# Causal mask of layer A's attention: added by VectorE in PSUM in place of TensorE, with the second sum of each step issued behind the next step's mask

## The chip, the cores and the metric

The kernel runs on one core of a Trainium2 chip. The metric is the device time of one execution in microseconds (us); the time shown is the median of several runs. The engines have short names in the profile: PE is TensorE's matmul, PEld its weight load, DVE is VectorE, ACT is ScalarE, POOL is GpSimd and SP is SyncE, whose queue issues the DMAs here.

## The reference

A two-layer decoder trunk over 2048 tokens of width 1024 in float32. Layer A is forgetting attention: 16 heads of 64, causal softmax with a cumulative log forget gate as bias. Then come one shared K/V projection and layer B, a sliding-window attention with sinks. Only layer A's attention is touched by the change; cut to what matters:

```python
def fox_attention(q, k, v, log_f):
    c = jnp.cumsum(log_f, axis=1)
    ...
    def block(args):                      # 128 queries at a time
        idx, qi, ci = args
        logits = einsum('bqhd,bkhd->bhqk', qi, k) * HEAD_DIM ** -0.5
        logits = logits + ci[..., :, None] - c_k[..., None, :]
        causal = k_pos[None, :] <= q_pos[:, None]
        logits = jnp.where(causal, logits, -jnp.inf)
        p = jax.nn.softmax(logits, axis=-1)
        return einsum('bhqk,bkhd->bqhd', p, v)
# layer A: h = h + (o * silu(gate)) @ w_out_a
```

## The kernel before

Every float32 product is made of high and low parts: a value is split into a rounded part and the rest, and a product is the sum of two or three matmuls. So PE has several matmuls of 512 columns for each tile of each projection, and the other engines make the splits.

Layer A's attention is the function `attention_a`. Work is cut into 64 units, one for each head and each chunk `ch` of 512 queries (4 chunks). Scores are held transposed, with 128 keys on the partitions and up to 512 queries along the columns. A unit of chunk `ch` has 2*ch + 2 steps, and each step `p` treats two blocks of 128 keys; a head has 20 steps and all heads 320. In most steps both blocks are seen by all 512 queries. The last two steps of a unit hold the diagonal: step 2*ch has blocks of 512 and 384 columns, each with a triangle of 128 columns to be masked, and the last step has 256 and 128 columns in one PSUM tile, with two triangles masked together.

A step runs like this. `scores` issues two matmuls for each block into PSUM tiles `sc` (L995 and L996; three banks). In the two diagonal steps a further matmul adds the mask: the identity in bf16, `identb`, times the triangle `mask_s`, which holds -1e30 above the diagonal (L1005 twice in step 2*ch, L1001 once, 256 columns wide, in the last step). ACT takes the exponentials into `pf` (L1011, L1002; tag `st`, four slots), casts them to the high part (L1014), and POOL subtracts that for the low part (L1015). For the softmax's denominator the exponentials are summed over the keys on DVE: a PSUM bank `ac` (one slot) starts as a copy of the unit's first block (L1018, ACT), and each further block is added to it by DVE (L1024), the two blocks of a step one after the other. Behind the last step of a unit `sums` reduces `ac` (L912, DVE), and five steps later `recips` (L921 to L928) forms reciprocals.

Around this other work is threaded. `values` (L1039, PE) runs three steps behind the scores, in one PSUM bank `pa`, with the high and the low part. `max_pieces` computes the running row maxima of the following head: PE writes a piece into one of two PSUM banks `mx` (L950), and DVE reduces it (L963) or, on the diagonal, adds a bf16 mask in place and reduces (L958). There are 40 pieces a head, two in each step, one before the scores and one behind them. `gate` is a filler: it feeds the matmuls of the gate projection (L1081, bank `pb`) whose weights come by DMA through SP into `wr`, and whose products are finished on DVE and ACT (L1092 to L1094).

The order in the text is the program's order. The framework plans each engine's queue: an instruction that its cost model takes as ready may go ahead of one that is listed earlier and is not ready; among ready ones the earlier listed goes first. `keep_in_program_order` pins an instruction behind all listed before it on its engine. Each engine runs its queue in order.

Of the kernel before, what the change touches and what calls it, by code (L numbers as in the profile page):

```python
# [14 lines left out]
BF16 = mybir.dt.bfloat16  # L15
# [3 lines left out]
ALU = mybir.AluOpType  # L19
# [4 lines left out]
P = 128  # L24
# [76 lines left out]
def f_(ap):  # L101
    return ap.bitcast(F32)
# [51 lines left out]
class Trunk:  # L154
# [56 lines left out]
    def constants(self):  # L211
        nc, cp, a = self.nc, self.const, self.a

        def select(view, src, pattern, base, cm, fill):
            nc.gpsimd.affine_select(
                out=view, in_=src, pattern=pattern, compare_op=ALU.is_ge,
                fill=fill, base=base, channel_multiplier=cm,
            )

        def tile_(name, shape, dt=F32):  # L220
            return cp.tile(shape, dt, name=name, tag=name)

        idle = self.sb("sq", [P, CH], F32R)
        nc.vector.memset(f_(idle), 0.0)
        ps = self.ps("pb", [P, CH])
        for i in range(IDLE):
            self.tc.keep_in_program_order(
                nc.tensor.matmul(ps, idle[:, :P], idle, start=i == 0, stop=i == IDLE - 1)
            )

        self.ones = tile_("ones", [P, P])
        nc.gpsimd.memset(self.ones, 1.0)
        self.tri = tile_("tri", [P, P])
        select(self.tri, self.ones, [[1, P]], 0, -1, 0.0)
        self.ident = tile_("ident", [P, P])
        select(self.ident, self.tri, [[-1, P]], 0, 1, 0.0)

        self.fold = tile_("fold", [P, 32])
        nc.vector.tensor_tensor(self.fold, self.ident[:, :32], self.ident[:, 32:64], ALU.add)
        for c in (64, 96):  # L240
            nc.vector.tensor_tensor(self.fold, self.fold, self.ident[:, c : c + 32], ALU.add)
        nc.vector.tensor_single_scalar(self.fold, self.fold, 2.0, ALU.mult)
        self.identb = tile_("identb", [P, P], BF16)
        nc.vector.tensor_copy(self.identb, self.ident)

        self.mask_s = tile_("mask_s", [P, P], BF16)
        nc.gpsimd.memset(self.mask_s, 0.0)
        select(self.mask_s, self.mask_s, [[1, P]], 0, -1, NEG)

        self.band = tile_("band", [P, 2, P], BF16)  # L250
        nc.gpsimd.memset(self.band[:, 0], 0.0)
        select(self.band[:, 0, :], self.band[:, 0, :], [[-1, P]], 0, 1, NEG)
        nc.vector.tensor_tensor(self.band[:, 1], self.tri, self.ident, ALU.subtract)

        self.loads = []
        warm = tile_("warm", [P, 1])
        nc.scalar.activation(warm, self.ones[:, :1], AF.Sqrt)

        def vector(name, n, views):
            t = tile_(name, [P, n])  # L260
            for rows, src in views:
                self.loads.append((t[rows], src))
            return t

        def column(name, src, n):
            return vector(name, n, [(slice(0, P), src.rearrange("(t p) -> p t", p=P))])

        def pair_column(name, src):
            col = src.rearrange("(p o) -> p o", o=1)
            return vector(name, 1, [(slice(0, HD), col), (slice(HD, P), col)])  # L270

        def row(name, src, n):
            return vector(name, n, [(slice(0, P), src.to_broadcast([P, n]))])

        self.g_a = column("g_a", a["norm_a_g"][0], NDT)
        self.bf = row("bf", a["b_forget"], H)
        self.g_qa = pair_column("g_qa", a["qnorm_a_g"][0])
        self.g_ka = pair_column("g_ka", a["knorm_a_g"][0])
        self.g_b = column("g_b", a["norm_b_g"][0], NDT)
        self.g_kv = column("g_kv", a["kv_norm_g"], NDT)  # L280
        self.g_qb = pair_column("g_qb", a["qnorm_b_g"][0])
        self.g_kb = pair_column("g_kb", a["knorm_b_g"])
        self.sink = row("sink", a["sinks"], H)
        self.gq16 = row("gq16", a["qnorm_b_g"][:, :ROT], ROT)
# [579 lines left out]
    def attention_a(self, op):  # L864


        nc, tc, d = self.nc, self.tc, self.d
# [15 lines left out]
        heads, state = {}, {}  # L883
        units = [(h, ch) for h in range(H) for ch in range(NCH)]
# [24 lines left out]
        def sums(u):  # L909

            h, ch = units[u]
            nc.vector.tensor_reduce(  # L912
                part[h // 2 % 2][:, h % 2, ch, :], state[u][0].rearrange("p (b i) -> p b i", i=32),
                AX.X, ALU.add, apply_transpose=True,
            )
# [55 lines left out]
        def blocks(ch, p):  # L971

            if p < 2 * ch:
                return [(2 * p, 0, 512, 0), (2 * p + 1, 0, 512, 512)]
            if p == 2 * ch:
                return [(2 * p, 0, 512, 0), (2 * p + 1, 128, 384, 512)]
            return [(2 * p, 256, 256, 0), (2 * p + 1, 384, 128, 256)]

        def scores(n, u, p):
            h, ch = units[u]  # L980
            ka, kb, qa, qb, v, _ = heads[h]
            bl = blocks(ch, p)
            diag, last = p >= 2 * ch, p > 2 * ch

            tiles = [self.ps("sc", [P, CH]) for _ in range(1 if last else 2)]
            tw = bl[1][3] + bl[1][2]
            pf = self.sb("st", [P, 1024])
            ph, pl = pht[:, n % 4, :], plt[:, n % 4, :]
            for n_, (k, q0, w, off) in enumerate(bl):
                qs = slice(ch * CH + q0, ch * CH + q0 + w)  # L990
                ks = slice(k * P, (k + 1) * P)
                ps = tiles[0 if last else n_]
                o0 = off if last else 0
                o = ps[:, o0 : o0 + w]
                nc.tensor.matmul(o, ka[:, ks], qa[:, qs], start=not (last and n_), stop=False)  # L995
                nc.tensor.matmul(o, kb[:, ks], qb[:, qs], start=False, stop=not diag)  # L996

            if last:
                o = tiles[0].rearrange("p (b q) -> p b q", b=2)[:, :, :P]
                m = self.mask_s.unsqueeze(1).to_broadcast([P, 2, P])  # L1000
                nc.tensor.matmul(o, self.identb, m, start=False, stop=True)  # L1001
                nc.scalar.activation(pf[:, :tw], tiles[0][:, :tw], AF.Exp, scale=HD**-0.5)  # L1002
            else:
                for n_, ps in enumerate(tiles if diag else ()):
                    mm = nc.tensor.matmul(  # L1005
                        ps[:, :P], self.identb, self.mask_s, start=False, stop=True
                    )
                    if n_:
                        tc.keep_in_program_order(mm)
                for ps, (k, q0, w, off) in zip(tiles, bl):  # L1010
                    nc.scalar.activation(  # L1011
                        pf[:, off : off + w], ps[:, :w], AF.Exp, scale=HD**-0.5
                    )
            nc.scalar.copy(ph[:, :tw], pf[:, :tw])  # L1014
            nc.gpsimd.tensor_tensor(pl[:, :tw], pf[:, :tw], f_(ph[:, :tw]), ALU.subtract)  # L1015
            if p == 0:
                state[u] = [self.ps("ac", [P, CH]), None]
                nc.scalar.copy(state[u][0], pf[:, :CH])  # L1018
            acc = state[u][0]
            for n_, (k, q0, w, off) in enumerate(bl):  # L1020
                if p == 0 and n_ == 0:
                    continue
                a_ = acc[:, q0 : q0 + w]
                nc.vector.tensor_tensor(a_, a_, pf[:, off : off + w], ALU.add)  # L1024
            if last:
                sums(u)
            return (u, p, ph, pl)

        def values(item):
# [123 lines left out]
        for n, (u, p) in enumerate(steps):  # L1153
# [26 lines left out]
            if n in PREP_AT:  # L1180
                op.load(PREP_AT.index(n), ("qn", "wh", "qn", "wl"))
                op.prepare(PREP_AT.index(n), nc.gpsimd)
        op.load(2, ("qn", "wh", "qn", "wl"))
        gate_bank, weight_slots = "mx", cycle(["st", "wr"])
        for item in pending:
# [463 lines left out]
```

## Time and profile before

| | us |
|---|---|
| median of 3 runs (2434.35 to 2436.96) | 2435.06 |
| the profiled execution | 2432.95 |
| its span, first to last instruction | 2431.0 |
| PE busy, of the span | 2406.9 |
| DVE busy | 1730.6 |
| ACT busy | 1260.0 |
| POOL busy | 997.5 |

The granted TensorE clock was 1.00. Busy time of an engine is the time in which at least one of its instructions has its span open; matmuls overlap, so PE's busy time is no measure of how near it is to its peak, and the distance between the starts of two neighbours says what the first takes of the engine. A row of a timeline gives start, length, engine, line, operation and tiles, with a count where neighbours were merged, and in brackets the idle time ahead of it. A row of the chain or of the waits names a line of the kernel as printed above. A row of windows gives the stretch, its length, the busy time of PE, PEld, DVE, ACT and POOL with the number of instructions in brackets, the clock and the DMA's share and rate.

### The profile page before, as it was taken

The numbers are of one execution on the slowest core, as the hardware profiler recorded it, in microseconds if no ns is written. First come the engines' busy times: TensorE is split into PE (matmuls) and PEld (weight loads), VectorE is DVE, ScalarE is ACT, GpSimd is POOL, SyncE is SP. The second block draws the span as 40 slices with busy tenths as digits, with TensorE's granted clock in tenths as the row PEclk, the third lists the DMA queues.
The fourth block names the chain that finished last, engine by engine and source line by source line (L and its number), as shares of the span: only waits on it lengthen the run. The fifth ranks groups of instructions, "written<-read, shape, count | busy, mean of one in ns | idle before, by whom it ended". The sixth has DMA issues, their size and how long they took to land.

```text
span 2431.0 us, 36257 instructions
## 1 busy us (share of the span) xinstructions
PE 2406.9 (99%) x11960; PEld 2027.7 (83%) x11960; DVE 1730.6 (71%) x4086; ACT 1260.0 (52%) x2504; POOL 997.5 (41%) x642
## 2 busy tenths in 40 slices
PE   9999999999999999999999999999999999999999
PEld 7888899987888788888888878888888888788887
DVE  7756657735999888899988865556666523777775
ACT  5433324323878778777878761135332312555554
POOL 0000000011878777777878852200011000477775
PEclk9999999999999999999999999999999999999999
DMA  6656555677654755575466559965433425655552
GB/s 185 208 168 190 154 155 166 197 235 232 179 165 127 211 155 147 150 219 167 127 196 178 166 153 312 299 225 162 120 107 105 139 72 157 179 178 180 180 180 74
DMA packets 351484, 419.25 MB, mean 172 GB/s; under 512 B 64896, under 2 KB 248224, under 8 KB 345120
## 3 DMA queue, kind: packets, MB, share of 16 engines
q1 hardware_dynamic: 351296, 416.93, 57.5%
q8 instruction: 95, 1.56, 0.3%
q14 instruction: 93, 0.76, 0.1%
HBM read 265.30 MB, written 151.40 MB: 171 GB/s over the span
## 4 chain that ended last, share of the span: by engine, by line
PE 90%; DVE 4%; DMA 3%; ACT 2%; issue 1%; POOL 1%; SPq 0%; ACTq 0%; DVEq 0%; POOLq 0%
PE b L774 30%; PE pa L1039 10%; PE pb L1081 7%; PE b L1266 5%; PE pb L1479 5%; PE sc L995 5%; PE sc L996 5%; PE mx L950 5%; PE pb L737 3%; PE b L737 3%; PE pa L1409 2%; PE b L1330 2%; PE pb L358 1%; DVE wl L502 1%; PE pa L358 1%
## 5 line engine op out<-in xcount | busy, mean ns | idle before, releaser
L774 PE MATMUL b<-wh,big 128*128 128x512 f32 (+3 forms) x2560 | 772.0, 375 | 0.7 <-ACT wh L501 0.7
L1015 POOL TENSOR_TENSOR big<-st,big 128x1024 fp32r<-128x1024 f32 (+1 forms) x320 | 655.5, 2068 | 238.7 <-ACT big L1014 157.2
L774 PEld LDWEIGHTS b<-wh,big 128*128 128x128 f32 x2560 | 470.9, 188 | 72.0 <-ACT wh L501 2.5
L774 PE MATMUL b<-wl,big 128*128 128x512 f32 (+3 forms) x1280 | 474.4, 371 | 0.8 <-DVE wl L502 0.8
L1024 DVE TENSOR_TENSOR ac<-ac,st 128x512 f32<-128x512 f32 (+3 forms) x576 | 353.1, 613 | 51.0 <-ACT st L1011 25.5
L1011 ACT ACTIVATE st<-sc 128x512 f32<-128x512 f32 (+1 forms) x512 | 273.4, 582 | 117.7 <-PE sc L996 50.1
L1039 PE MATMUL pa<-big 128*128 128x512 f32 (+3 forms) x1280 | 319.2, 366 | 0.6 <-POOL big L1015 0.6
L1014 ACT CAST big<-st 128x1024 fp32r<-128x1024 f32 (+1 forms) x320 | 295.2, 923 | 8.5
L774 PEld LDWEIGHTS b<-wl,big 128*128 128x128 f32 x1280 | 241.5, 189 | 37.4 <-DVE wl L502 5.2
L1039 PEld LDWEIGHTS pa<-big 128*128 128x128 f32 x1280 | 229.4, 190 | 38.4 <-POOL big L1015 1.9
L963 DVE TENSOR_REDUCE mt<-mx 128x1 f32<-128x384 f32 (+1 forms) x360 | 214.7, 599 | 30.5 <-PE mx L950 28.1
L510 ACT ACTIVATE sq<-b,r 128x512 f32<-128x512 f32 (+2 forms) x128 | 77.7, 607 | 304.2 <-PE b L774 304.2
L995 PE MATMUL sc<-big 128*128 128x512 f32 (+3 forms) x640 | 233.1, 368 | 1.1 <-DVE st L557 1.1
L996 PE MATMUL sc<-big 67*128 67x512 f32 (+3 forms) x640 | 229.8, 367 | 0.0
L950 PE MATMUL mx<-big 66*128 66x512 f32 (+2 forms) x600 | 225.3, 380 | 0.2
L1081 PE MATMUL pb<-wh,wr 128*128 128x512 f32 x488 | 177.6, 396 | 3.4 <-DMA wr<-wg 3.3
L512 DVE TENSOR_REDUCE sm<-sq 128x8 f32<-128x512 f32 (+2 forms) x128 | 74.9, 585 | 141.3 <-ACT sq L510 141.1
L874 POOL MEMSET rot<- 128x512 bf16 x1 | 0.5, 524 | 419.8 <-PE pb L358 419.8
L1378 POOL TENSOR_TENSOR big<-big,tri 128x1024 fp32r<-128x1024 f32 x60 | 143.8, 2397 | 69.2 <-DVE big L1375 64.3
L958 DVE CUSTOM_DVE_ANT_0 mx<-mx,rot 128x384 f32<-128x384 f32 (+2 forms) x240 | 147.1, 618 | 17.5 <-PE mx L950 16.2
L995 PEld LDWEIGHTS sc<-big 128*128 128x128 f32 x640 | 121.9, 190 | 22.7 <-DVE st L557 1.5
L996 PEld LDWEIGHTS sc<-big 67*128 67x128 f32 x640 | 122.1, 191 | 19.2
(285 smaller groups left out, 4131.3 us busy)
## 6 DMA issues: line engine op xcount, KB each, us to landing
wr<-wg SPq DMA_DIRECT2D x62, 512.0 KB, 4.5
va<-st SPq DMA_DIRECT2D x32, 512.0 KB, 4.7
ka<-st SPq DMA_DIRECT2D x64, 256.0 KB, 3.8
ut<-big SPq DMA_DIRECT2D x16, 1024.0 KB, 7.0
big<-ka SPq DMA_DIRECT2D x16, 1024.0 KB
big<-qa SPq DMA_DIRECT2D x16, 1024.0 KB, 8.2
qb<-st SPq DMA_DIRECT2D x64, 256.0 KB, 3.8
big<-qb SPq DMA_DIRECT2D x16, 1024.0 KB, 6.3
```

What stands on the lines that cost most here:

```text
L774: nc.tensor.matmul(ps[:, :n], u[tb // 4][:, dt, us], W[k][dt], start=(dt == 0 and i == 0), stop=(dt == NDT - 1 and i == 2),)
L950: mm = nc.tensor.matmul(ps, qb[:66, i * P : (i + 1) * P], kb[:66, k0:k1], start=True, stop=True,)
L958: nc.vector.tensor_tensor_reduce(out=ps, in0=ps, in1=mask_m[:, 512 - w :], scale=1.0, scalar=NEG, op0=ALU.add, op1=ALU.max, accum_out=f_(o),)
L963: nc.vector.reduce_max(o, ps, axis=AX.X)
L995: nc.tensor.matmul(o, ka[:, ks], qa[:, qs], start=not (last and n_), stop=False)
L996: nc.tensor.matmul(o, kb[:, ks], qb[:, qs], start=False, stop=not diag)
L1011: nc.scalar.activation(pf[:, off : off + w], ps[:, :w], AF.Exp, scale=HD**-0.5)
L1014: nc.scalar.copy(ph[:, :tw], pf[:, :tw])
L1015: nc.gpsimd.tensor_tensor(pl[:, :tw], pf[:, :tw], f_(ph[:, :tw]), ALU.subtract)
L1024: nc.vector.tensor_tensor(a_, a_, pf[:, off : off + w], ALU.add)
L1039: nc.tensor.matmul(pv[:, q0 : q0 + w], v[:, k, :], src[:, off : off + w], start=(p == 0 and n_ == 0 and i == 0), stop=(last and n_ == 1 an ...
L1081: nc.tensor.matmul(ps, w[:, dt // 2 % 2, wk, dt % 2, :], us[dt][uk], start=(dt == 0 and i == 0), stop=(dt == NDT - 1 and i == 2),)
```

## The change

The two mask matmuls of step 2*ch and the one of the last step go, and with them `identb` and the copy that made it. In their place DVE adds `mask_s` to the score tiles in PSUM, in place, ahead of the exponentials: two additions of 128 columns, and one over both triangles (256 columns). The second block's sum of a step, and the unit's reduction `sums`, are no longer issued in the step itself but put on a list, `to_add`, which `add_up` empties in the next step behind its masks and ahead of its exponentials; what is left after the last step is added after the loop. The first block's sum stays in its own step. The step's second score matmul now ends its accumulation where the mask did.

```diff
-        self.identb = tile_("identb", [P, P], BF16)
-        nc.vector.tensor_copy(self.identb, self.ident)
...
+        to_add = []
+
+        def add_up():
+
+            for u, p, bl, pf in to_add:
+                k, q0, w, off = bl[1]
+                a_ = state[u][0][:, q0 : q0 + w]
+                nc.vector.tensor_tensor(a_, a_, pf[:, off : off + w], ALU.add)
+                if p > 2 * units[u][1]:
+                    sums(u)
+            to_add.clear()
...
-                nc.tensor.matmul(o, kb[:, ks], qb[:, qs], start=False, stop=not diag)
+                nc.tensor.matmul(o, kb[:, ks], qb[:, qs], start=False, stop=not last or n_ == 1)
 
             if last:
                 o = tiles[0].rearrange("p (b q) -> p b q", b=2)[:, :, :P]
                 m = self.mask_s.unsqueeze(1).to_broadcast([P, 2, P])
-                nc.tensor.matmul(o, self.identb, m, start=False, stop=True)
+                nc.vector.tensor_tensor(o, o, m, ALU.add)
+                add_up()
                 nc.scalar.activation(pf[:, :tw], tiles[0][:, :tw], AF.Exp, scale=HD**-0.5)
             else:
-                for n_, ps in enumerate(tiles if diag else ()):
-                    mm = nc.tensor.matmul(
-                        ps[:, :P], self.identb, self.mask_s, start=False, stop=True
-                    )
-                    if n_:
-                        tc.keep_in_program_order(mm)
+                for ps in tiles if diag else ():
+                    nc.vector.tensor_tensor(ps[:, :P], ps[:, :P], self.mask_s, ALU.add)
+                add_up()
...
-            acc = state[u][0]
-            for n_, (k, q0, w, off) in enumerate(bl):
-                if p == 0 and n_ == 0:
-                    continue
-                a_ = acc[:, q0 : q0 + w]
+            if p:
+                k, q0, w, off = bl[0]
+                a_ = state[u][0][:, q0 : q0 + w]
                 nc.vector.tensor_tensor(a_, a_, pf[:, off : off + w], ALU.add)
-            if last:
-                sums(u)
+            to_add.append((u, p, bl, pf))
...
+        add_up()
         op.load(2, ("qn", "wh", "qn", "wl"))
```

## The prediction

> **What bounds the kernel now.** I read the page's totals first, then the stretch that holds layer A's attention, then the chain of waits there, and only then single instructions.
>
> ```profile
> span 2431.0 us, 36257 instructions
> PE 2406.9 (99%) x11960; PEld 2027.7 (83%) x11960; DVE 1730.6 (71%) x4086; ACT 1260.0 (52%) x2504; POOL 997.5 (41%) x642
> PE 90%; DVE 4%; DMA 3%; ACT 2%; issue 1%; POOL 1%; SPq 0%; ACTq 0%; DVEq 0%; POOLq 0%
> ```
>
> The page names PE, but matmul spans overlap, so 99% alone proves little. The score matmuls of this attention run from about 592 to 1434 us. The table of windows for that stretch (its length first, then each engine's busy time), and the chain of waits by line for the same stretch:
>
> ```profile
> 592.00:1434.00 842.00, 836.70 (x4100) 694.38 (x4099) 734.93 (x1604) 669.75 (x1059) 666.62 (x329) 1.00 0.58 167
> ```
>
> ```profile
> by line: PE pa L1039 28.9%; PE pb L1081 19.8%; PE sc L995 15.0%; PE sc L996 14.9%; PE mx L950 14.8%; DMA wr<-wg 2.3%; PE sc L1005 0.9%; PE sc L1001 0.9%; ACT big L1014 0.4%; issue 0.3%; ACT st L1011 0.3%; POOL big L1015 0.3%; PE sc L921 0.2
> ```
>
> Some 95% of the chain is PE, and the mask matmuls (L1005, L1001) are on it with 0.9% each, together 1.8% of 842 = 15 us. The engine behind PE is DVE: 734.93 of 842 us busy, 107 us idle. It is the one that the change loads.
>
> **The mask matmuls that go.** 64 units (16 heads, 4 chunks) have one step with two masks of 128 columns and one last step with one of 256. PE's timeline over one such pair of steps (start, length, last the count):
>
> ```profile
> 1006.36 0.34 PE L996 MATMUL sc<-big 67*128 67x384 f32 x1
> 1006.54 0.28 PE L1005 MATMUL sc<-mask_s,identb 128*128 128x128 bf16 x2
> 1006.64 0.42 PE L950 MATMUL mx<-big 66*128 66x384 f32 x1
> 1006.90 1.07 PE L1039 MATMUL pa<-big 128*128 128x512 f32 x4
> ...
> 1008.26 0.34 PE L950 MATMUL mx<-big 66*128 66x384 f32 x1
> 1008.43 0.28 PE L995 MATMUL sc<-big 128*128 128x256 f32 x1
> ...
> 1008.74 0.27 PE L996 MATMUL sc<-big 67*128 67x128 f32 x1
> 1008.85 0.28 PE L1001 MATMUL sc<-mask_s,identb 128*128 128x256 bf16 x1
> 1008.89 0.42 PE L950 MATMUL mx<-big 66*128 66x384 f32 x1
> 1009.15 1.09 PE L1039 MATMUL pa<-big 128*128 128x512 f32 x4
> ```
>
> Starts say what an instruction takes of PE. The pair of masks holds 1006.54 to 1006.64, 0.10 us. The 384-column matmul after it then takes 0.26 us to the next start (1006.64 to 1006.90), where the same shape without a mask ahead takes 0.17 (1008.26 to 1008.43): another 0.09. So a pair costs 0.18 to 0.19 us, taken as 0.18. The 256-column mask costs 0.04 (1008.85 to 1008.89) and again 0.09 behind it, 0.13 in sum, of which I take 0.12, as each start is rounded to 0.01. 64 x (0.18 + 0.12) = 19.2 us. The chain gives 15 us from the other side. Both agree that PE really pays; I take 19.2, since no other line has that PE time to give.
>
> **The mask additions that come.** 128 additions of 128 columns and 64 of 256 go to DVE, in place in PSUM, with the bf16 mask as second operand. No such instruction is in the trace; the nearest are the causal maxima L958 (in place in PSUM, bf16 mask too) and the sums L1024 (PSUM and SBUF). Groups by form: count, busy us, mean ns.
>
> ```profile
> L958 DVE CUSTOM_DVE_ANT_0 mx<-mx,rot 128x128 f32<-128x128 f32 x15 | 4.4, 296 | 4.1 <-PE mx L950 3.5 <-DMA big<-ka 0.5
> L958 DVE CUSTOM_DVE_ANT_0 mx<-mx,rot 128x256 f32<-128x256 f32 x15 | 6.9, 459 | 0.0
> L1024 DVE TENSOR_TENSOR ac<-ac,st 128x128 f32<-128x128 f32 x64 | 19.2, 300 | 1.0
> ```
>
> And DVE's timeline, for what such widths take of the engine:
>
> ```profile
> 1025.83 0.42 DVE L1024 TENSOR_TENSOR ac<-ac,st 128x256 f32<-128x256 f32 x1
> 1026.15 0.68 DVE L963 TENSOR_REDUCE mt<-mx 128x1 f32<-128x512 f32 x1
> ...
> 1026.75 0.29 DVE L1024 TENSOR_TENSOR ac<-ac,st 128x128 f32<-128x128 f32 x1
> 1026.95 0.69 DVE L958 CUSTOM_DVE_ANT_0 mx<-mx,rot 128x512 f32<-128x512 f32 x1
> ```
>
> By length: 128 x 0.296 + 64 x 0.459 = 67 us. By what they hold up: the next DVE instruction starts 0.20 us after a 128-column one (1026.75 to 1026.95) and 0.32 after a 256-column one (1025.83 to 1026.15), so 128 x 0.20 + 64 x 0.32 = 46 us. These are the two ends for DVE. I take 46, because the rows show DVE starting the next instruction 0.1 us before the last one's span ends.
>
> The Trainium skill, "VectorE: DVE Perf Modes", section "The DRAIN you can't avoid", speaks against that choice and so against the change: the next operation, it says, starts only when the pipeline is empty. By that rule an addition would cost its whole span and DVE 67 us. The rows above disagree for neighbours that don't wait for each other (0.20 us against a span of 0.29), so the measurement decides; a mask that the next DVE instruction had to wait for would follow the page.
>
> What covers the 46 us? DVE is off the path as long as the running maxima free their two PSUM banks in time: a piece (L950) needs its bank reduced two pieces earlier. Where DVE is late, PE waits; the waits that say so, and the one cover of the moved reduction (in total us, times, longest):
>
> ```profile
> PEld mx L950 <- DVE mt L963: 2.8, 12, 0.4
> PEld mx L950 <- DVE m L958: 2.4, 8, 0.4
> PEld mx L950 <- DVE mt L958: 1.0, 4, 0.3
> ACT ac L1018 <- DVE part L912: 0.2, 1, 0.2
> PEld pa L1039 <- POOL big L1015: 1.9, 4, 0.7
> ACT st L1011 <- PE sc L1005: 46.1, 48, 1.9
> ```
>
> Today that is 24 waits, 6.2 us. How much it becomes is the unknown of this case, and I bound it by DVE's idle time. After the change the stretch would be 842 - 19 = 823 us and DVE busy 735 + 46 = 781, idle 42 instead of 107, 2.5 times less. If the waits grow as idle shrinks, 6.2 x 2.5 = 15.8, which is 9.6 more. By the long end, idle is 823 - 802 = 21, the waits 6.2 x 5.1 = 31.6, 25 more. The low end is no growth at all: DVE's lateness also shrinks with every PE wait, and the rest of its idle time lies in gaps that the masks could fill. I don't go below nothing: the same banks get more work in front of them. I take 10.
>
> **Latency of the masked steps.** The exponentials (L1011, L1002) waited for the mask matmul and now wait for the addition. In the step above the first tile's scores end 0.40 after their start at 1005.94; DVE is then in a maximum until 1006.68 and the two additions would end near 1007.1, against 1006.86 for the exponential's start before (timelines below). Some 0.2 us late on ACT, then on the cast, POOL and, three steps on, the value matmuls. What is late next would be L1039, which waits for POOL 1.9 us in four places today: 64 units could add at most a little there, as three steps of about 2.6 us lie between. I cost it at nothing; without that cover it would be 128 x 0.2 = 26 us.
>
> ```profile
> 1005.94 0.40 PE L996 MATMUL sc<-big 67*128 67x512 f32 x1
> ...
> 1006.08 0.69 DVE L958 CUSTOM_DVE_ANT_0 mx<-mx,rot 128x512 f32<-128x512 f32 x1
> ...
> 1006.86 0.98 ACT L1011 ACTIVATE st<-sc 128x512 f32<-128x512 f32 x2 [1.05 <-PE sc L1005]
> ```
>
> **The wait that is added.** An addition at the head of DVE's queue waits for the scores of its own tile, and behind it stand the deferred sum, the maxima and the gate's products. PE waits for the maxima only through the two banks, so a wait of under about a microsecond at the head is absorbed in the row above; it is inside the 10 us.
>
> **The moved second sum.** Second sums, and with a unit's last one the reduction L912, now follow the next step's masks in DVE's order. They issue no DMA and pass no other queue than DVE's; SP's and POOL's order is as before. Behind them wait: the `st` buffer of their step (four slots, held one step longer), the single `ac` bank, whose next user is the copy L1018 (waits for L912 once today, 0.2 us), and the reciprocals, five steps later. Steps without a mask lose little: a sum whose exponential is done may be planned ahead of a piece whose matmul isn't, wherever the program lists it. I cost this at nothing, with the copy as cover: it stands behind two exponentials and a cast on ACT. Dropping the identity's bf16 copy is one DVE instruction at the start, nothing.
>
> **Sum.** The profiled execution took 2432.95 us (span 2431.0), 2.1 below the median of 2435.06. 2432.95 - 19.2 + 10 = 2423.8; on the median's footing 2425.9, so 2426. With no new waits it is 2435.1 - 19.2 = 2416, with the long end 2435.1 - 19.2 + 25 = 2441.
>
> **The rivals.**
>
> *DVE becomes the bound of the masked steps* (the other side). Windows of those two steps, length, PE, PEld, DVE, ACT, POOL:
>
> ```profile
> 1005.71:1008.43 2.72, 2.72 (x15) 2.23 (x14) 2.35 (x6) 1.64 (x4) 2.39 (x1) 1.00 0.00 0
> 1008.43:1010.99 2.56, 2.56 (x15) 2.23 (x15) 2.29 (x6) 1.39 (x3) 2.04 (x1) 1.00 0.12 1
> ```
>
> With the additions DVE has 2.35 + 0.40 = 2.75 and 2.29 + 0.32 = 2.61 us to do, against 2.72 and 2.56 now: if nothing is carried over into neighbouring steps, a unit is 0.03 + 0.05 longer, 64 x 0.08 = 5 us, 2440. By whole spans (2 x 0.296 and 0.459) it is 0.22 + 0.19, 26 us, 2461. It decides once DVE's arrears exceed what two banks cover. For it speaks that both steps stand beside each other; against it that PE's waits for DVE are 6 us in 842 and that arrears can be made up later. This is also what the page's rule would lead to. Chance 0.19.
>
> *The gain is eaten*: head-of-queue waits cost as much as PE gives. 128 masked steps x 0.15 us = 19 us: 2435. For it speaks that the scores come on PE right before the additions, so DVE has little else ready; against it, that maxima and sums fill the queue. Chance 0.16.
>
> *The change does nothing for time* because the attention is paced by something else, the gate's weights (DMA wr<-wg, 2.3% of the chain, 19 us): then the freed PE time turns into longer waits for them, 2435. That share is spread over few places and PE idles only 842 - 836.7 = 5.3 us. Chance 0.05.
>
> **How the numbers follow.** Forecast: faster, 2426, chance 0.60, its own range 2416 to 2430. The two cases around no change have 0.21, DVE as the bound 0.19. About 0.2% (4.9 us) is what a measurement of this kernel tells from no change; so faster 0.60, same 0.21, slower 0.19. For 8 times in 10 the range must reach into the rivals: from 2414 (all of 19 and a little more, for what the shorter stretch does to the transfers) to 2446, which takes in the low part of DVE as the bound.
>
> **What would show it.** Right: L1001 and L1005 gone, the attention stretch 9 to 19 us shorter, the 384-column pieces behind the masks at 0.17 spacing, DVE's busy time in it near 781, PE's waits at L950 for DVE between 6 and 20 us. Wrong: these waits at 30 us or more, or waits at the score matmuls for ACT or at L1039 for POOL that are not there now; DVE busy beyond 800 of the stretch; or new additions longer than 0.30 and 0.46 us.

## The result, and the profile after

The change made the kernel slower: 2455.15 us (median of four runs, 2451.54 to 2458.26) against 2434.7 in the same comparison, a ratio of 1.0085 with a 95% interval of 1.007 to 1.010. The forecast was 2426, with a range that ended at 2446. The profiled execution took 2452.87 us.

The page's totals, and the windows row of layer A's attention (columns as in the prediction):

```profile
span 2451.2 us, 35992 instructions
PE 2407.5 (98%) x11768; PEld 2023.2 (83%) x11768; DVE 1764.0 (72%) x4277; ACT 1243.5 (51%) x2504; POOL 1002.2 (41%) x642
```

```profile
592.00:1434.00 842.00, 817.57 (x3832) 674.59 (x3833) 759.05 (x1777) 638.23 (x1039) 652.62 (x323) 0.99 0.58 164
```

The 192 mask matmuls are gone and 192 additions have come. PE's busy time is what it was, over a span that is 20 us longer, and in the same 842 us of the attention PE gets through 3832 instructions in place of 4100, of which some 190 were masks. From the first to the last score matmul the attention takes 853.4 us, before 835.0; from the last score matmul to layer A's output projection 20.9, before 16.5. The rest is 2.6 us shorter. So the whole loss, 20.2 us by the two profiles, lies in this stretch and its end.

The additions, grouped by form (count, busy us, mean ns of one; then the idle time ahead of them), and rows of what PE and ACT wait for in the stretch (total us, times, longest):

```profile
L1015 DVE TENSOR_TENSOR sc<-sc,mask_s 128x128 f32<-128x128 f32 x126 | 33.5, 300 | 3.1 <-PE sc L1005 3.0
L1010 DVE TENSOR_TENSOR sc<-sc,mask_s 128x256 f32<-128x256 f32 x63 | 27.1, 430 | 0.8 <-PE sc L1005 0.8
```

```profile
PE pa L1043 <- POOL big L1022: 15.7, 24, 1.8
PEld pa L1043 <- POOL big L1022: 32.1, 43, 2.0
PEld sc L1004 <- ACT st L1018: 5.2, 11, 1.2
PEld mx L947 <- DVE m L955: 0.5, 2, 0.2
PEld mx L947 <- DVE mt L960: 0.2, 1, 0.2
ACT st L1018 <- DVE sc L1015: 56.7, 35, 3.4
ACT st L1012 <- DVE sc L1010: 36.6, 32, 2.9
```

Each addition is as short as forecast, and DVE is not full (759 of 842). The wait that was forecast, for DVE at the causal pieces, is not there: it even fell from 6.2 us to under 1. In its place PE waits for POOL's low part at the value matmuls, 32 us in PEld's rows where there were 1.9. The last two rows say why POOL is late: ACT stands 93 us in front of additions that are not done. One unit's last step on the timeline (start, length, last the idle time ahead and its releaser):

```profile
1307.27 0.28 PE L1005 MATMUL sc<-big 67*128 67x128 f32 x1
...
1307.57 0.69 DVE L983 TENSOR_TENSOR ac<-ac,st 128x512 f32<-128x512 f32 x1
...
1308.16 0.54 DVE L960 TENSOR_REDUCE mt<-mx 128x1 f32<-128x384 f32 x1
...
1308.63 0.69 DVE L1029 TENSOR_TENSOR ac<-ac,st 128x512 f32<-128x512 f32 x1
...
1309.23 0.68 DVE L955 CUSTOM_DVE_ANT_0 mx<-mx,rot 128x512 f32<-128x512 f32 x1
...
1309.83 0.46 DVE L1010 TENSOR_TENSOR sc<-sc,mask_s 128x256 f32<-128x256 f32 x1
...
1310.69 0.49 ACT L1012 ACTIVATE st<-sc 128x384 f32<-128x384 f32 x1 [1.15 <-PE sc L1005]
```

The last step's scores are ready at 1307.55. Four DVE instructions stand ahead of their addition in the queue, so it starts at 1309.83, 2.3 us late, and ends at 1310.29; the exponential starts at 1310.69, and its row puts the last part of the wait down to a later score matmul. Over all units the additions start a median of 1.9 us (the first of step 2\*ch) and 1.8 us (last step) behind their scores, and what the low part has to spare ahead of its value matmul falls from 3.35 to 0.58 us and from 3.96 to 1.39.

To compare kernels I use one accounting: for each PE instruction of the attention, the time to the next start less what that width takes undisturbed (0.233 us for 512 columns, 0.178 for 384, 0.120 for 256, 0.083 for 128; 799.8 us in all kernels), put down to the instruction that starts late. What stretches at a granted clock of 0.5 cost is estimated as half their length and has a column of its own. All in us:

| kernel | attention | masks | values | pieces | gate products | scores | half clock |
|---|---|---|---|---|---|---|---|
| before | 835.0 | 11.6 | 8.3 | 1.3 | 5.1 | 8.9 | 0 |
| the change | 853.4 | 0 | 30.4 | 2.3 | 5.4 | 10.3 | 5.1 |
| masks alone, newly planned | 856.6 | 0 | 35.8 | 1.8 | 5.9 | 9.8 | 3.4 |
| the change, PE in before's order | 849.7 | 0 | 7.0 | 16.0 | 4.2 | 14.2 | 8.5 |
| before, PE in the change's order | 855.3 | 11.0 | 13.1 | 11.4 | 7.2 | 6.1 | 6.7 |
| all queues in before's order: no mask | 826.9 | 0 | 3.5 | 3.4 | 9.3 | 9.2 | 1.7 |
| – additions on time | 844.2 | 0 | 4.8 | 19.6 | 8.2 | 11.8 | 0 |
| – additions set back | 916.5 | 0 | 6.7 | 62.4 | 9.0 | 24.9 | 13.7 |
| – additions of 8 columns, no mask | 831.8 | 0 | 3.7 | 8.3 | 9.9 | 9.9 | 0 |
| – last step's additions only | 842.6 | 6.9 | 6.6 | 8.3 | 8.6 | 10.7 | 1.7 |

Half clock behind an idle PE:

```profile
1315.00:1318.40 3.40, 1.64 (x10) 1.29 (x9) 1.77 (x4) 1.29 (x2) 3.32 (x4) 0.96 0.36 102
1318.40:1321.80 3.40, 3.40 (x10) 2.83 (x10) 1.77 (x4) 1.78 (x3) 3.40 (x2) 0.50 0.44 92
```

```profile
1317.95 0.75 PE L1043 MATMUL pa<-big 128*128 128x256 f32 x3 [1.76 <-POOL big L1022]
...
1319.03 0.63 PE L1005 MATMUL sc<-big 67*128 67x512 f32 x1
```

PE waits 1.76 us for POOL, and in the 3.4 us that follow the column of the clock shows 0.50 and a matmul of 512 columns lasts 0.63 us in place of 0.40. The change has three stretches of 3.4 us at this clock in its attention, before has none.

### The profile page after: what moved, and what is told of

Same layout as the page of the kernel before. It is cut to its first block, busy times and chain, and to the rows that moved or that the text cites. A ratio compares the mean times of both kernels' runs of the same rounds, so it can differ in the third digit from the quotient of the medians.

```text
span 2451.2 us, 35992 instructions
## 1 busy us (share of the span) xinstructions
PE 2407.5 (98%) x11768; PEld 2023.2 (83%) x11768; DVE 1764.0 (72%) x4277; ACT 1243.5 (51%) x2504; POOL 1002.2 (41%) x642
## 5 line engine op out<-in xcount | busy, mean ns | idle before, releaser
L1043 PE MATMUL pa<-big 128*128 128x512 f32 (+3 forms) x1280 | 353.8, 369 | 21.4 <-POOL big L1022 18.5
L1018 ACT ACTIVATE st<-sc 128x512 f32<-128x512 f32 (+1 forms) x512 | 284.7, 590 | 133.1 <-DVE sc L1015 56.9
L771 PEld LDWEIGHTS b<-wl,big 128*128 128x128 f32 x1280 | 241.3, 189 | 35.8 <-DVE wl L499 3.5
L983 DVE TENSOR_TENSOR ac<-ac,st 128x512 f32<-128x512 f32 (+1 forms) x320 | 190.0, 594 | 18.0 <-ACT ac L1025 16.1
L1029 DVE TENSOR_TENSOR ac<-ac,st 128x512 f32<-128x512 f32 (+1 forms) x256 | 161.4, 631 | 6.9 <-ACT st L1012 3.3
```

Source lines behind the costliest of these rows:

```text
L771: nc.tensor.matmul(ps[:, :n], u[tb // 4][:, dt, us], W[k][dt], start=(dt == 0 and i == 0), stop=(dt == NDT - 1 and i == 2),)
L1018: nc.scalar.activation(pf[:, off : off + w], ps[:, :w], AF.Exp, scale=HD**-0.5)
L1043: nc.tensor.matmul(pv[:, q0 : q0 + w], v[:, k, :], src[:, off : off + w], start=(p == 0 and n_ == 0 and i == 0), stop=(last and n_ == 1 an ...
```

## The experiments

Ratios are to the kernel before in the same comparison, with 95% intervals.

### Parts of the change

**Masks on DVE, each sum in its own step.**

```diff
 # against the change
-            if p:
-                k, q0, w, off = bl[0]
+            for n_, (k, q0, w, off) in enumerate(bl):
+                if p == 0 and n_ == 0:
+                    continue
...
-            to_add.append((u, p, bl, pf))
+            if last:
+                sums(u)
```

> The mask goes to VectorE, both sums stay in their own step. Theory A (lateness: the additions stand behind a full VectorE queue, so exponentials, POOL's low part and the value matmuls come late): still slower than before, ratio 1.004 to 1.015, and the additions start 1.5 us or more after their scores. Rival C (the deferral of the second sum did the harm): faster than before, 0.993 to 0.997.

**Only the second sum behind the next step's mask; masks stay on PE.**

```diff
 # against before
             if last:
...
                 nc.tensor.matmul(o, self.identb, m, start=False, stop=True)
+                add_up()
...
+            to_add.append((u, p, bl, pf))
```

> The mask stays on TensorE; only the second sum and the unit's reduction are issued in the next step, behind its mask matmuls. Theory A: no change, 0.998 to 1.002. Rival C (the deferral did the harm): slower by 10 to 20 us, 1.004 to 1.008.

**Both sums behind the next step's mask.**

```diff
 # against the change, in add_up
-                k, q0, w, off = bl[1]
+                for n_, (k, q0, w, off) in enumerate(bl):
```

> The change with both sums of a step issued behind the next step's masks. Theory A (lateness of the masked exponentials because the additions stand behind other VectorE work): with the first sums out of the way too, additions start earlier than the change's 1.9 us behind their scores; 5 to 20 us faster than the change, 2435 to 2450. Rival D (the planned order of the engines' queues is what makes the additions late): still 1.5 us late or more, within 5 us of the change.

Masks alone: 2455.64, 1.0104 (1.0088 to 1.0120), the whole loss. The moved sum alone: 2438.24, 1.0027 (1.0017 to 1.0038), a small loss, with 5.7 us more in front of the gate products. Both sums moved: 2467.94, 1.0145 (1.0132 to 1.0159), 13 us slower than the change, which neither theory had; the additions still start 1.9 and 2.0 us late. So the move of the masks is the cause, and the moved sum is neither a remedy nor the culprit.

### The hop, the load and the mask matmuls, each by itself, newly planned

**Load: zeros added on `ac`, as many and as wide as the masks, off the exponentials' path.**

```diff
 # against before
             if last:
+                nc.vector.tensor_tensor(o, o, z, ALU.add)        # o: 256 columns of ac
                 sums(u)
+            elif diag:
+                for n_ in range(2):
+                    o = acc[:, n_ * P : (n_ + 1) * P]
+                    nc.vector.tensor_tensor(o, o, mask_m[:, :P], ALU.add)
```

> The kernel before, with 128 additions of 128 columns and 64 of 256 more on VectorE in the diagonal steps, in place in PSUM with a bf16 operand as in the change, but of zeros onto the accumulator of the sums, so that no exponential waits for them. Rival B (capacity: 46 to 67 us more VectorE work is what costs): slower by 20 to 40 us, since the mask matmuls are still there, 1.008 to 1.016. Theory A (lateness of the exponentials): the work alone costs little, 0 to 8 us, 1.000 to 1.003.

**Hop: 8 columns of zeros added to the masked score tiles, masks still on PE.**

```diff
 # against before
+                for ps in tiles if diag else ():
+                    nc.vector.tensor_tensor(ps[:, :8], ps[:, :8], mask_m[:, :8], ALU.add)
```

> The kernel before, with an addition of zeros by VectorE on the first 8 columns of each masked score tile behind the mask matmul (two in the step 2*ch, one in the last): the exponentials wait for VectorE as in the change, but VectorE's added work is small. Theory A: slower by 15 to 40 us, 1.006 to 1.016, with exponentials some 2 us after their scores in the diagonal steps. Rival B (capacity): 192 instructions of at most 0.1 us, within 8 us of before, 1.000 to 1.003.

**No mask at all.**

```diff
 # against before
-                nc.tensor.matmul(o, self.identb, m, start=False, stop=True)
-                nc.scalar.activation(pf[:, :tw], tiles[0][:, :tw], AF.Exp, scale=HD**-0.5)
+                nc.scalar.activation(pf[:, :tw], tiles[0][:, :tw], AF.Exp, scale=1e-4)
...
```

> The kernel before without the mask matmuls and without any mask; the exponential's scale is 1e-4 so that the unmasked scores stay finite. It prices the mask matmuls alone. By the prediction's term 19 us faster than before (ratio 0.992); if the freed TensorE time turned into waits for something else, 0 to 8 us.

Load: 2538.08, 1.0438 (1.0424 to 1.0453); hop: 2440.04, 1.0033 (1.0021 to 1.0046); no mask: 2425.58, 0.9977 (0.9968 to 0.9985). The hop lies between the two theories: its additions start 0.8 us behind their scores and take 0.17 us each, not at most 0.1. The other two don't fit any sum of durations. Some 66 us of additions (128 of 301 ns, 64 of 434) that no exponential waits for cost 107 us, and taking out what I had priced at 19.2 us gave 6. In all three the framework had planned the queues anew, which is the next question.

### The order of the queues

**Every matmul of the attention pinned in program order, in before and in the change.**

```diff
 # in both
-                nc.tensor.matmul(o, ka[:, ks], qa[:, qs], start=not (last and n_), stop=False)
+                tc.keep_in_program_order(nc.tensor.matmul(o, ka[:, ks], qa[:, qs], ...))
```

> The kernel before with TensorE's matmuls of this attention pinned in program order (scores, masks, pieces, values, gate). It is the control of the next one. Its values are in groups of four mostly already, so within 10 us of before: 0.997 to 1.004.

> The changed kernel with the same pins, so that TensorE's order is that of the control without its masks. Rival D in the form that TensorE's order did it (its value matmuls are split into ones and twos by the plan): no slower than the control, 5 to 19 us faster. Theory A, or VectorE's order: slower than the control by 5 to 25 us.

The pinned before takes 2482.92, 1.0220 (1.0200 to 1.0241), the pinned change 2472.48, 1.0166 (1.0152 to 1.0180): with one order of PE's matmuls for both, the change is 10 us faster, though the control is 51 us slower than before, not within 10, and both lose to the gate's weights and to half clock. In the pinned change the additions start 0.2 and 0.3 us behind their scores. That made the order the suspect.

**PE's queue held in a listed order.** Each matmul of the attention is collected by kind (`queued`) and tied behind the one ahead of it in a list; the other queues are planned anew.

```diff
+        for kind in re.sub(r"(\d+)(.)", lambda m: m[2] * int(m[1]), PE_ORDER):
+            mm = queued[kind].pop(0)
+            if prev is not None:
+                tc.add_manual_dep(mm.ins, prev.ins.name, ..., reason="order")
+            prev = mm
```

The change with before's list:

> The changed kernel, with TensorE's matmuls of this attention forced into exactly the order that the kernel before has on that queue, its mask matmuls left out. Theory D (TensorE's planned order is what made the change slow; the additions themselves are affordable): 2414 to 2430, faster than before, ratio 0.993 to 0.999, additions within 0.7 us of their scores. Theory A or B (VectorE's queue or its capacity): 2445 or more, additions 1.5 us or more late.

Before with the change's list, the mask matmuls behind their scores:

> The kernel before, masks on TensorE, with its matmuls forced into the order that the changed kernel has on TensorE's queue, each mask matmul right behind its step's last score matmul. Theory D: slower by 15 to 40 us, 2450 to 2470. Theory A or B: within 8 us of before, 2425 to 2440.

No mask with before's list:

> The kernel before with no mask at all (exponential's scale 1e-4, scores left unmasked), TensorE otherwise in the order of before. It prices the mask matmuls with nothing planned anew: by the prediction 19 us, 2412 to 2416; if the freed time turns into waits, 2420 to 2430.

The load on `ac` with before's list:

> The kernel before with the 192 additions of zeros on VectorE that no exponential waits for (as in the load-only run), TensorE forced into the order of before, masks included. Rival B (capacity): slower by 20 us or more, as far as VectorE's work exceeds what the stretch holds. Theory D (the load-only run lost its 107 us to a newly planned order): 2430 to 2445.

The change in before's PE order: 2445.81, 1.0043 (1.0026 to 1.0059), which fits neither theory: the additions start 0.4 and 0.6 us behind their scores and nothing is won. Its values wait no more (7.0 us in the table), and the waits at the pieces that were forecast come:

```profile
PEld mx L992 <- DVE mt L1007: 15.4, 29, 1.2
PEld mx L992 <- DVE mt L1002: 3.9, 9, 1.0
```

Before in the change's PE order: 2450.78, 1.0075 (1.0063 to 1.0087), 19 us without one addition. The load in before's PE order: 2462.35, 1.0122 (1.0107 to 1.0136); 77 of its 107 us had been order. But no mask in before's PE order came out at 2450.39, 1.0075 (1.0062 to 1.0088), slower than newly planned (2425.58), with 24.4 us in which PE waits for the gate's weights. Holding one queue while four others are planned anew does not separate the causes. So next I held all five.

### All five queues in before's order

The planned position of each instruction of before on PE, DVE, ACT, POOL and SP is a list; each instruction is tied behind the one ahead of it. Additions are inserted in DVE's list where, by before's trace, their scores are ready. Nothing else moves: in the traces of these kernels every other instruction of the five engines runs in before's order.

```diff
+def as_planned_before(tc, added=()):
...
+        queue = [mine[k] for k in order]
+        if key == "DVE" and extra:
+            for at, ins in reversed(list(zip(np.maximum(numbers("anchors"), 1009), extra))):
+                queue.insert(at, ins)
+        for before, ins in zip(queue, queue[1:]):
+            tc.add_manual_dep(ins, before.name, ..., reason="order")
```

**No mask:**

> Leaves the causal mask of layer A out altogether (and scales the scores by 1e-4 so that the exponentials stay finite); the queues of TensorE, VectorE, ScalarE, GpSimd and SyncE are all held in the order planned for the kernel before. So it takes away the 192 mask matmuls and replans nothing. If the prediction's term for the mask matmuls is right (19.2 us of TensorE's time at these places) and only the newly planned order ate it, this runs at 2412 to 2418 us, attention 815 to 820 us long from its first to its last score matmul. If TensorE's time in attention is not what sets the end (gate weights that land late, a clock that is halved when TensorE idles), it stays within 10 us of before, as the kernel without a mask and with a new plan did (2425.6), with the difference standing in the waits for the gate weights.

**The additions, on time:**

> The change's additions on VectorE, none on TensorE, second sums in their own steps; all five queues are held in the order planned for the kernel before, and each of the 192 additions stands in VectorE's queue at the point where, by the trace of before, its scores are ready. If the loss of the change comes from the newly planned order (theory order), this is faster than before: 2416 to 2428 us, additions starting under 0.6 us behind their scores, TensorE's waits for GpSimd at the value matmuls under 3 us. If the additions themselves cost the loss (the hop through VectorE and its 65 us of work, rival), it stays at 2440 us or more with 10 us or more of waits at the value matmuls or at the causal pieces, although no other instruction has moved.

**The additions, set back by one or two places:**

> As the kernel with the additions in the old queues, with each addition set further back in VectorE's queue: behind what started up to 1.7 us after its scores were ready in the trace of before (one or two instructions, sums and causal pieces), though never behind its own step's sum. Every other instruction keeps its place. If the late start of the additions is what costs the change its time, this is 10 to 25 us slower than the kernel with the additions on time, with the waits for GpSimd at the value matmuls back (10 us or more). If it is rather the order of the other queues (value matmuls split into ones and twos, causal pieces moved), it stays within 5 us of it.

No mask: 2422.5, 0.9962 (0.9950 to 0.9975). Additions on time: 2443.8, 1.0047 (1.0032 to 1.0062). Set back: 2517.16, 1.0345 (1.0330 to 1.0360).

The first settles the mask matmuls. In the table masks and what follows them at the values give 16.4 us (11.6, and 8.3 to 3.5), against 19.2 forecast. But 8.3 return: 4.2 ahead of the gate products, 2.1 at the pieces, 1.7 half clock, 0.3 at the scores. What is left is 8.1 in the attention and 10 in the median. The waits for the gate's weights and at the pieces in this kernel, and then for the weights in before:

```profile
PE pb L1175 <- DMA wr<-wg: 7.8, 6, 2.9
PEld pb L1175 <- DMA wr<-wg: 10.0, 6, 3.3
PEld mx L1051 <- DVE mt L1064: 4.6, 16, 0.4
...
PEld mx L1051 <- DVE m L1059: 2.5, 8, 0.5
PEld mx L1051 <- DVE mt L1059: 1.8, 7, 0.3
```

```profile
PE pb L1081 <- DMA wr<-wg: 3.3, 4, 1.3
PEld pb L1081 <- DMA wr<-wg: 4.9, 5, 1.7
```

The second refutes my theory that the new order was the whole cause. Additions 0.34 and 0.49 us behind their scores, values as before (3.2 us and more to spare), no other instruction moved, and still 21 us slower than without them. The page's shares of the chain, then PE's waits at the pieces, then what DVE waits for:

```profile
PE 77%; DVE 10%; DMA 4%; ACT 4%; issue 3%; POOL 1%; SPq 0%; DVEq 0%; ACTq 0%; POOLq 0%
```

```profile
PEld mx L1051 <- DVE mt L1064: 16.6, 41, 0.8
PEld mx L1051 <- DVE mt L1059: 13.8, 24, 1.5
PEld mx L1051 <- DVE m L1059: 2.9, 9, 0.5
DVE ac L1138 <- ACT st L1125: 22.9, 40, 1.6
DVE ac L1138 <- ACT ac L1132: 15.5, 21, 1.8
DVE mx L1059 <- PE mx L1051: 10.3, 15, 1.8
DVE mt L1064 <- PE mx L1051: 6.9, 18, 0.8
```

DVE is on the chain with 10%, where the page of before has 4%. The same rows of before for DVE:

```profile
DVE mt L963 <- PE mx L950: 28.1, 62, 1.0
DVE ac L1024 <- ACT st L1011: 25.5, 45, 1.3
DVE mx L958 <- PE mx L950: 16.2, 22, 2.5
DVE ac L1024 <- ACT ac L1018: 16.2, 21, 2.4
```

Read the two fences side by side. DVE's waits for PE's pieces fall from 44.3 to 17.2 us: the additions fill them, and that is the slack there was. Its waits for ACT's exponentials stay (41.7 and 38.4, and 3.2 more in a row left out): the sums stand in an in-order queue, and an addition ahead of them doesn't bring the exponential nearer. What the slack doesn't hold comes out as PE's wait for a bank: 33.3 us in PEld's rows, 8.9 without a mask and 6.2 before.

In the third I had the effect right in sign and wrong in size and place. One or two places further back cost 73 us, and not at the values but at the pieces (62.4 in the table): the exponentials are late, DVE then stands in front of its own sums, and behind these stand the reductions that free the banks.

```profile
DVE ac L1138 <- ACT st L1125: 30.9, 59, 1.3
DVE ac L1138 <- ACT st L1117: 29.9, 48, 0.6
DVE ac L1138 <- ACT ac L1132: 29.0, 25, 2.1
PEld mx L1051 <- DVE mt L1059: 41.0, 46, 2.0
```

Here the additions start a median of 1.2 us (the first of step 2\*ch) and 2.1 us (last step) behind their scores. In the newly planned change they are about as late (1.9 and 1.8 us), and it loses far less, and at the values instead. So lateness alone doesn't set the price; what stands behind the late sums in the new order seems to, but no run separates that.

**Is it DVE's work, or the round trip?**

Round trip kept, work cut (no mask, 8 columns of zeros added to the score tiles):

```diff
-                        nc.vector.tensor_tensor(ps[:, :P], ps[:, :P], self.mask_s, ALU.add)
+                        nc.vector.tensor_tensor(ps[:, :8], ps[:, :8], mask_m[:, :8], ALU.add)
```

> As the kernel without a mask in the old queues (scores scaled by 1e-4, all five queues in the order planned for before, 2422.5), plus the change's 192 additions at the same places of VectorE's queue, but only 8 columns of zeros wide. The exponentials still wait for VectorE, and VectorE still waits for the scores, but the work is some 0.17 us each, 29 to 32 us in all, in place of 62. Before has 44 us in which VectorE waits for TensorE at the causal pieces (28.1 + 16.2). If VectorE's work is what overflows this slack (theory work), 29 us fit in: 2422 to 2432 us, under 8 us of TensorE's waits at the pieces. If the round trip through VectorE costs the time (theory hop), it stands near the kernel with the full additions: 2438 us or more, 15 us of such waits.

Work kept, round trip cut (no mask, additions in place on an SBUF tile):

```diff
+                    o, m = self.mask_s[:, :P], mask_m[:, :P]
+                    self.added.append(nc.vector.tensor_tensor(o, o, m, ALU.add))
```

> The other half of the pair: no mask, all queues as before, and 192 additions at the same places of VectorE's queue with 128 and 160 columns, but in place on a tile in SBUF that nobody else reads, so that no exponential waits for them and they wait for no score. Some 0.3 us each, 59 us in all. Theory work: 59 us exceed the 44 us of slack, so 12 to 20 us of waits at the pieces, 2436 to 2444 us. Theory hop: nobody waits for them in time, 2422 to 2430 us and under 6 us of waits at the pieces.

A third of the masks:

```diff
 # against before: only the last step's mask
-                nc.tensor.matmul(o, self.identb, m, start=False, stop=True)
+                self.added.append(nc.vector.tensor_tensor(o, o, m, ALU.add))
```

> A third of the change: only the masks of the last step of each unit go to VectorE (64 additions of 256 columns, 27.5 us), TensorE keeps the 128 masks of the diagonal steps, second sums in their own steps, all five queues in the order planned for before. Theory work: 27.5 us fit into the 44 us of slack, so the waits at the pieces grow by under 6 us, and TensorE is rid of a third of what the masks cost it (16 us before what its idle time turned into): 2424 to 2432 us, a little faster than before. Theory hop: the exponentials of the last steps run 0.9 us later as with all additions, 5 us of waits at the pieces or more: 2433 to 2438 us.

Round trip kept: 2427.86, 0.9988 (0.9978 to 0.9998), 5 us above no mask in place of 21; the additions 0.27 and 0.33 us behind their scores, nearly as in the full kernel. So in this order the round trip by itself costs at most 5 us; the other 16 come with the width of the additions, 63 us busy in place of 30.6. The waits at the pieces are 16 us where I had expected under 8, but 8.9 of them are there without any addition, and the full width had 33. The groups of the narrow ones, and PE's waits at the pieces:

```profile
L1122 DVE TENSOR_TENSOR sc<-sc,rot 128x8 f32<-128x8 f32 x128 | 19.7, 177 | 3.2 <-PE sc L1110 2.9
L1116 DVE TENSOR_TENSOR sc<-sc,rot 128x8 f32<-128x8 f32 x64 | 10.9, 171 | 0.7 <-PE sc L1110 0.7
```

```profile
PEld mx L1051 <- DVE mt L1064: 6.8, 21, 0.6
PEld mx L1051 <- DVE mt L1059: 6.4, 14, 1.2
...
PEld mx L1051 <- DVE m L1059: 2.9, 8, 0.8
```

Work kept went wrong as a test: 2629.3, 1.0813 (1.0792 to 1.0833), because the stand-in was not the same work. One addition of 128 columns took 1.36 us on average in SBUF, not 0.30 as in PSUM, 216 us in all (what the groups show of both forms), and 167 us of the attention ran at half clock, which cost up to 84 us. It says that this much work on DVE bounds the stretch; it can't say what 59 us would cost.

```profile
L1121 DVE TENSOR_TENSOR mask_s<-mask_s,rot 128x128 f32<-128x128 f32 x126 | 171.3, 1360 | 1.3
L1115 DVE TENSOR_TENSOR mask_s<-mask_s,rot 128x160 f32<-128x160 f32 x63 | 45.0, 714 | 0.0
```

A third of the masks: 2435.19, 1.0014 (1.0005 to 1.0022), no gain, and in the range that I had given the other theory. The table shows it: masks and values give 6.4 us, pieces take 7.0, gate products 3.5, scores 1.8, half clock 1.7. With 27.4 us of additions the pieces cost as much as with 30.6 us in the kernel with 8 columns. So the 44 us are no reserve that fills up before anything is felt: some 30 us of work cost 5 to 7 us at the pieces, 63 us cost 16 to 18. No version that applies the mask by additions beat the kernel before.

## Why the prediction was wrong, step by step

**The mask matmuls that go (19.2 us).** Mechanism right, size a little off. Start by start against the kernel without a mask in the same order, a pair of masks cost a median of 0.184 us, as forecast; the 256-column mask cost 0.075, not 0.12, since most of the 0.09 behind it is there without a mask too: the 384-column piece behind the last step's scores takes a median of 0.23 us there, not 0.17. In the table PE gave up 16.4 us. Half of it came back as waits at once, above all for the gate's weights. That is the third rival's mechanism, to which I gave 0.05: it took 4 to 5 us here, not all. So the term was worth 8 us in the attention.

**The mask additions that come.** Right: 300 and 430 ns (bounds 296 and 459), and the next DVE instruction starts a median of 0.20 and 0.33 us after them, so 46 and not 67 us is what they hold up. On the page "VectorE: DVE Perf Modes" of the Trainium skill, section "The DRAIN you can't avoid", the rule of the empty pipeline is not what these additions show; the section's own exception, that a next operation which is not held starts earlier, is. The prediction took the section without that exception.

**What covers the 46 us (10 us of waits).** This is the step that failed first. I scaled the waits by DVE's idle time, 107 us before, as if all of it could be filled. 41.7 of it are waits of the sums for ScalarE, which the additions did not shorten; only 44.3 are waits for pieces. With all queues unchanged the waits at the pieces grow by 27 us in PEld's rows and 18.3 in the table, not 10, near the long end of 25 that I had kept for the range. With both terms as measured the kernel with unchanged queues is already 9 us slower in its attention (16.4 given up, 8.3 and 17.3 taken), not 9 faster. That is the rival that DVE becomes the bound of the masked steps, which I gave 0.19 and 2440 to 2461: the additions on time in unchanged queues (2443.8) fit it in time and in mechanism. The change (2455) lies in the same range by luck, since its waits for DVE at the pieces are under 1 us.

**"SP's and POOL's order is as before", and DVE's order but for the sums.** False, and the rest of the loss. In the trace of the change POOL's order is nearly kept (8 of 642 instructions moved), but 74 of SP's 1499, 172 of ACT's 2504 and 326 of DVE's 4085 (moved sums among them) stand in another order, and so do PE's matmuls: one more engine between scores and exponentials made the framework plan all queues anew. In its plan the waits at the pieces are gone (2.3 us), but the additions stand behind sums and pieces.

**Latency of the masked steps (nothing).** I took one step's DVE queue and found 0.2 us; the additions start 1.9 us late. I had named what would come next, L1039 waiting for POOL, with 26 us if its cover went. It went: the values lost 22.1 us more than before, and half clock 5.1. With both sums in their own step and the same additions, the new plan costs 12.4 us in the attention (856.6 against 844.2). Late additions in the old order left the values at 6.7 us, so the loss there belongs to the lateness and the new order together; how it divides between them, and which rule of the planner chose this order, is not shown.

**The moved second sum (nothing).** Small, but not nothing: 0.27% by itself, nothing to be seen on top of the masks.

Of the signs that I had listed, the two for "wrong" that name ACT at the scores and POOL at L1039 are what the profile after shows; DVE over 800 is not.

## What to carry to other kernels

Don't count an engine's idle time as room for new work: split it by what ends each wait, and count at most the waits that end on the engine that you relieve; even those were not free here, where 27 us of work beside 44 us of such waits cost 7. And an instruction put between two engines changes a planned order, which can cost as much as the instruction; hold every queue in the old order once to see which of the two you are measuring. Time taken from the bounding engine is not all won: here half of it went to the next waits.

## What the runs showed of the hardware

In the SBUF test an addition of 128 columns took a median of 0.29 us when GpSimd was idle at its start (35 of 128), and otherwise up to 4.26: where a GpSimd subtraction was running, it ended 0.147 us after the end of that, almost without spread (0.145 to 0.154 in 91 of 92 cases).

```profile
1002.98 7.92 POOL L1128 TENSOR_TENSOR big<-st,big 128x1024 fp32r<-128x1024 f32 x4 [1.69 <-ACT big L1127]
1003.55 1.99 DVE L1121 TENSOR_TENSOR mask_s<-mask_s,rot 128x128 f32<-128x128 f32 x1
```

The additions with one operand in PSUM took 0.30 beside the same subtractions. The Trainium skill, "SBUF — State Buffer", section "Who interferes with whom", says that a VectorE instruction with two SBUF inputs contends with a GpSimd instruction that reads SBUF, and that the shared ports are an exclusive lock; this run agrees.

PE's clock went to 0.50 for stretches of 3.4 us. In the attention of the change two of the three followed aligned stretches of 3.4 us in which PE had idled 1.76 and 1.78 us; the third came right behind the first, with PE busy all through. Other stretches there, with 1.29 us or less of idle time, kept the full clock, but in the kernel with the additions set back half clock also followed one with 1.30, so these runs show no sharp threshold. The Trainium skill, "TensorE: Matmul & The Clock Gate", section "What's actually happening", puts the fall behind an idle window of about 3.4 us; here a window that was idle for half of its length was enough. At some 1.7 us a stretch, by the estimate above, it adds to each wait that is long.
